# A bidirectional recurrence network on one core: where two conditioning rows are loaded, and which instructions are held to their place

## The chip, the cores and the metric

The kernel runs on one core of one Trainium2 chip. A core has five instruction streams that run beside each other: TensorE (PE, matrix products; its weight loads are listed as PEld), VectorE (DVE), ScalarE (ACT), GpSimd (POOL) and SyncE (SP), which here only issues transfers. Each engine takes its own instructions strictly in the order of the program that was built, and waits at an instruction until the semaphores it names have come. The metric is the device time of one execution in microseconds (us).

## The reference

Two layers of a network are applied to 128 context tokens and 512 latent tokens with the same weights. Context tokens are modulated by the conditioning vector `c_ctx`, latent tokens by `c`. One layer:

```
mod = silu(cond) @ ada_w + ada_b                 # six vectors of 1024: shift, scale, gate, twice
h   = rmsnorm(x, norm_mix) * (1 + sc_m) + sh_m
proj = h @ w_in                                   # 1024 x 4608, nine parts
o   = [4 gated-recurrence heads | 4 retention heads], both directions, head norm, gate
x   = x + g_m * (o @ w_out)
h   = rmsnorm(x, norm_ffn) * (1 + sc_f) + sh_f
gate, up = split(h @ w_up)                        # 1024 x 5632
x   = x + g_f * ((silu(gate) * up) @ w_down)      # 2816 x 1024
```

A final norm follows, and the states of the context tokens are returned. What matters here is the first line: the shifts and scales of both conditionings are 1024 long sums of `silu(cond)` times a column of `ada_w`.

## The kernel before

All 640 tokens stay on the chip. A product in fp32 is made of three products in the rounded type: each weight tile of 128x1024 is loaded raw (`Stream.load`, L65, by SP), its rounded part `wh` is made by ScalarE (L75) and the rest `wl` by VectorE (L76), and TensorE runs wh times the high part of the activations, wh times the low part and wl times the high part. Three raw buffers and four pairs of cut buffers run ahead of TensorE.

The work has stages: an early stage (called the boot here, `ada_first`, traced under a manual schedule, so in the order written), then for each layer the mixer (input projection with the heads' chains between it, `h0`, `a0`, ... in `ORDER`), `w_out`, and the FFN: eleven pairs of `w_up` units, the `w_down` product for 512 columns (L1053 to L1055) twice, eleven more pairs, `w_down` again.

The boot computes the first layer's first shift and scale, because nothing can start without them. Its steps: `load(i)` brings four tiles of `ada_w` (0.5 MB each) for i = 0 to 3; `cut(i, j)` splits tile j (L344 on ScalarE, L345 on VectorE); `mm(i, ..)` multiplies them with the two silu'd vectors (L355, or L358 unsplit); `rt(i)` turns the row to columns (L369), `fin(i)` adds the bias on VectorE (L376). Beside it the tokens are normalized: `xs`, `tr` (eight transposes, L586), `xc` (L395, a copy by ScalarE), then `full` (L408 and L410, scale and shift) and `split` (L414 and L415) make the activations `hT`, half by half, and the first projection products (`gw`, L624 to L626) run between.

All other shifts and scales come from `ada_cols`, for (layer 0, second norm) during layer 0's mixer and for layer 1 (both norms) during layer 0's FFN. It does not use TensorE. `ada_rows` loads both conditioning vectors, repeated on 128 partitions, as `srow` (two transfers of 0.5 MB), and ScalarE takes their silu (L515). Then for 16 tiles `adt` of the transposed `ada_w` (0.5 MB each, L527) VectorE runs two multiply-and-sums (L536), one for each conditioning, into one column of `modc`. `ada_cols` is a generator in a lane, `ada`: `Net.run` steps a lane each time the main work has added so much of an estimated cost (3.0 in the mixer, 4.0 in the FFN). A step decides where in the program an instruction is traced. After the boot the compiler's scheduler then orders each engine's stream anew by its own estimates, and may move an instruction ahead of older ones when it takes its inputs as ready. `pin` (`keep_in_program_order`) adds an edge that holds one instruction behind everything traced before it on its engine.

SP's transfers use eight completion semaphores in turn, so an issue also waits until the transfer eight before it has landed.

Of the kernel before, what the change touches and what calls it, by code (L numbers as in the profile page):

```python
# [13 lines left out]
AF = mybir.ActivationFunctionType  # L14
ALU = mybir.AluOpType
AX = mybir.AxisListType

P = 128
DM = 1024
# [36 lines left out]
class Stream:  # L56
# [5 lines left out]
    def load(self):  # L62
        src, kk, nn = self.slots[self.loaded]
        raw = self.net.rawp.tile([P, 1024], F32, tag="raw", name="raw")
        self.net.nc.sync.dma_start(out=raw[:, :kk * nn].rearrange("p (k n) -> p k n", k=kk), in_=src)  # L65
        self.raw[self.loaded] = (raw, kk, nn)
        self.loaded += 1

# [34 lines left out]
class Net:  # L103
# [218 lines left out]
    def ada_first(self):  # L322
# [89 lines left out]
        def split(t, hf):  # L412
            f, hi, lo = views(t, hf)
            nc.scalar.copy(hi, f)  # L414
            V.tensor_tensor(lo, f, hi.bitcast(F32), op=ALU.subtract)  # L415

        load(0)
        for t in range(NT):
            self.load_x(t)
        load(1)  # L420
        for _ in range(3):
            self.W.load()
        load(2)
        self.new_hT()
        for j in range(4):
# [83 lines left out]
    def ada_rows(self):  # L509
        a = self.a  # L510
        self.srow = self.const.tile([P, 2, DM], F32, name="srow")
        self.junk = self.const.tile([P, DM], F32, name="junk")
        for c, src in enumerate((a["c_ctx"], a["c"])):
            self.nc.sync.dma_start(out=self.srow[:, c], in_=bass.AP(src.tensor, src.offset, [[0, P], [1, DM]]))
        self.nc.scalar.activation(self.srow, self.srow, AF.Silu)  # L515

    def ada_cols(self, l, m, alloc):
        V = self.nc.vector
        if self.srow is None:
            self.ada_rows()  # L520
            yield
        tiles = [(which, j) for which in (1, 0) for j in range(KT)]

        def load(which, j):
            w = alloc("adt")
            row = 3072 * m + which * 1024 + j * P
            self.nc.sync.dma_start(out=w[:, :DM], in_=self.a["ada_t"][l, row:row + P])  # L527
            return w
        nxt = load(*tiles[0])
        for i, (which, j) in enumerate(tiles):  # L530
            w = nxt
            if i + 1 < len(tiles):
                nxt = load(*tiles[i + 1])
            yield
            for c in range(2):
                V.tensor_tensor_reduce(out=self.junk, in0=w[:, :DM], in1=self.srow[:, c], scale=1.0, scalar=0.0,  # L536
                                       op0=ALU.mult, op1=ALU.add,
                                       accum_out=self.modc[:, l, m, 1 - which, c, j:j + 1])
            yield
        self.mod_fin(l, m)  # L540

# [740 lines left out]
```

## Time and profile before

| | us |
|---|---|
| median of 3 runs (1847.05 to 1849.16) | 1849.0 |
| the profiled execution, whole | 1847.48 |
| its span, first to last instruction | 1845.7 |
| TensorE busy in the span | 1793.7 (97%) |
| VectorE busy | 1041.3 (56%) |
| ScalarE busy | 712.1 (39%) |

1.78 us of the profiled execution lie outside the span. Rows of the timeline give a start, a length and, in brackets, how long the engine had been idle before and what ended that idle time; a row with xN merges N instructions of one line. Matmuls overlap, so a row's length is more than the distance from one to the next. The stretches (windows) give each engine's busy time in a part of the span, the clock granted to TensorE as a share of 2.4 GHz, the busy share of the transfer engines, and GB/s. TensorE's clock has two levels, 1.2 and 2.4 GHz.

### The profile page before, as it was taken

How to read it: one execution, taken by the hardware profiler on the slowest of the kernel's cores; microseconds unless marked ns; L12 is line 12 of the kernel's file. 1: busy time of each engine (PE TensorE's matmuls, PEld its weight loads, DVE VectorE, ACT ScalarE, POOL GpSimd, SP SyncE). 2: the span in 40 equal slices, each digit the busy share in tenths (PEclk: the TensorE clock that was granted, in tenths of full speed). 3: DMA queues.
4: the chain of work that ended last, by engine and by line, in shares of the span. 5: the costliest groups of instructions: out<-in, count | busy, mean ns of one | idle time of the engine just before them, and what ended most of it. 6: DMA issues, size and time to landing. Idle time of an engine off the chain costs nothing.

```text
span 1845.7 us, 29294 instructions
## 1 busy us (share of the span) xinstructions
PE 1793.7 (97%) x12301; PEld 1719.7 (93%) x12301; DVE 1041.3 (56%) x1614; ACT 712.1 (39%) x1208; POOL 49.1 (3%) x59
## 2 busy tenths in 40 slices
PE   5999999999999999999999999999999999999998
PEld 3799999998999978999899999999899998899988
DVE  3889757864854986222366656587475522323234
ACT  5675645633522211222246555455352221122221
POOL 1000000000000000000000000000000000000000
PEclk7999999999999999999999999999999999999999
DMA  8424223222433654222222121322234322222221
GB/s 288 155 81 152 78 78 112 92 69 69 137 115 117 224 182 140 80 70 75 75 81 72 50 69 53 109 78 89 80 92 126 115 75 75 80 80 69 75 75 58
DMA packets 204612, 184.06 MB, mean 100 GB/s; under 512 B 6736, under 2 KB 172336, under 8 KB 204480
## 3 DMA queue, kind: packets, MB, share of 16 engines
q1 hardware_dynamic: 199584, 179.67, 30.8%
q10 hardware_dynamic: 4640, 2.43, 0.4%
q8 instruction: 96, 1.57, 0.4%
q0 software_dynamic: 256, 0.09, 0.1%
q14 instruction: 36, 0.29, 0.1%
HBM read 177.44 MB, written 4.72 MB: 99 GB/s over the span
## 4 chain that ended last, share of the span: by engine, by line
PE 78%; DVE 10%; DMA 4%; ACT 4%; issue 3%; SPq 1%; POOL 1%; DVEq 0%; POOLq 0%; ACTq 0%
PE gw L634 36%; PE ga L680 5%; PE ga L679 5%; PE ga L678 5%; PE ga L1053 5%; PE ga L1055 4%; PE ga L1054 4%; PE pl L771 3%; DMA adt<-in_ada_t 2%; DVE junk L536 2%; DVE wl L76 2%; PE gw L625 1%; PE gw L624 1%; PE gw L626 1%; PE ga L1032 1%
## 5 line engine op out<-in xcount | busy, mean ns | idle before, releaser
L634 PE MATMUL gw<-hT,wh 128*128 128x320 f32 x3712 | 702.0, 311 | 0.0
L634 PEld LDWEIGHTS gw<-hT,wh 128*128 128x128 f32 x3712 | 581.3, 188 | 1.1
L75 ACT CAST wh<-raw 128x1024 fp32r<-128x1024 f32 (+2 forms) x224 | 231.7, 1035 | 704.4 <-PE gw L634 267.1
L76 DVE TENSOR_TENSOR wl<-raw,wh 128x1024 fp32r<-128x1024 f32 (+2 forms) x224 | 269.4, 1204 | 357.3 <-ACT wh L75 357.1
L634 PE MATMUL gw<-hT,wl 128*128 128x320 f32 x1856 | 423.8, 309 | 0.0
L634 PEld LDWEIGHTS gw<-hT,wl 128*128 128x128 f32 x1856 | 310.4, 188 | 0.1
L678 PE MATMUL ga<-wh,hT 128*128 128x256 f32 x640 | 185.7, 290 | 0.0
L680 PE MATMUL ga<-wh,hT 128*128 128x256 f32 x640 | 181.4, 284 | 0.0
L679 PE MATMUL ga<-wl,hT 128*128 128x256 f32 x640 | 181.4, 283 | 0.0
L1053 PE MATMUL ga<-wh,act 128*128 128x512 f32 x330 | 130.2, 395 | 4.1 <-DVE xa L996 4.1
L1054 PE MATMUL ga<-wl,act 128*128 128x512 f32 x330 | 129.6, 393 | 0.0
L1055 PE MATMUL ga<-wh,act 128*128 128x512 f32 x330 | 128.8, 393 | 0.0
L536 DVE CUSTOM_DVE_ANT_0 junk<-adt,srow 128x1024 f32<-128x1024 f32 x96 | 117.8, 1227 | 18.5 <-DMA adt<-in_ada_t 17.0
L1104 DVE TENSOR_TENSOR sgf<-sgf,gw 128x640 f32<-128x640 f32 x44 | 36.1, 820 | 162.3 <-PE gw L634 162.3
L678 PEld LDWEIGHTS ga<-wh,hT 128*128 128x128 f32 x640 | 122.7, 192 | 0.3
L679 PEld LDWEIGHTS ga<-wl,hT 128*128 128x128 f32 x640 | 122.6, 192 | 0.3
L680 PEld LDWEIGHTS ga<-wh,hT 128*128 128x128 f32 x640 | 122.4, 191 | 0.0
L505 DVE SCALAR_TENSOR_TENSOR acc<-adw,sTt,acc 128x512 f32<-128x512 f32 x112 | 79.6, 747 | 23.0 <-DMA adw<-in_ada_w 22.7
L1053 PEld LDWEIGHTS ga<-wh,act 128*128 128x128 f32 x330 | 62.6, 190 | 18.6 <-DVE xa L996 6.0
L1055 PEld LDWEIGHTS ga<-wh,act 128*128 128x128 f32 x330 | 62.7, 190 | 13.3
L771 PE MATMUL pl<-X 128*128 128x128 f32 x560 | 72.3, 276 | 2.4 <-ACT X L758 2.3
L1054 PEld LDWEIGHTS ga<-wl,act 128*128 128x128 f32 x330 | 62.6, 190 | 12.5
(226 smaller groups left out, 2639.0 us busy)
## 6 DMA issues: line engine op xcount, KB each, us to landing
raw<-in_w_up SPq DMA_DIRECT2D x88, 512.0 KB, 3.8
raw<-in_w_in SPq DMA_DIRECT2D x72, 512.0 KB, 3.7
adt<-in_ada_t SPq DMA_DIRECT2D x48, 512.0 KB, 4.0
raw<-in_w_down SPq DMA_DIRECT2D x38, 512.0 KB, 3.7
adw<-in_ada_w SPq DMA_DIRECT2D x64, 256.0 KB, 2.9
adw<-in_ada_w SPq DMA_DIRECT2D x16, 512.0 KB, 7.0
raw<-in_w_out SPq DMA_DIRECT2D x16, 512.0 KB, 3.5
gate<-in_ada_b SPq DMA_DIRECT2D x8, 512.0 KB, 5.2
```

The source lines that it names most:

```text
L75: nc.scalar.copy(hi[:, :n], raw[:, :n])
L76: nc.vector.tensor_tensor(lo[:, :n], raw[:, :n], hi[:, :n].bitcast(F32), op=ALU.subtract)
L505: nc.vector.scalar_tensor_tensor(d, w, s, d, op0=ALU.mult, op1=ALU.add)
L536: V.tensor_tensor_reduce(out=self.junk, in0=w[:, :DM], in1=self.srow[:, c], scale=1.0, scalar=0.0, op0=ALU.mult, op1=ALU.add, accum_out=se ...
L634: mm(o, w[:, k], self.hT[:, d, k, sl], start=k == 0 and i == 0, stop=k == KT - 1 and i == 2)
L678: mm(o, a_hi, hi[:, j], start=i == 0, stop=False)
L679: mm(o, a_hi, lo[:, j], start=False, stop=False)
L680: mm(o, a_lo, hi[:, j], start=False, stop=i == nk - 1)
L771: nc.tensor.matmul(pl[:, i * P:(i + 1) * P], X[:, TOK + i * P:TOK + (i + 1) * P], X[:, i * P:(i + 1) * P], start=True, stop=True)
L1053: mm(o, a_hi, hi[:, j], start=i == 0, stop=False)
L1054: mm(o, a_hi, lo[:, j], start=False, stop=False)
L1055: mm(o, a_lo, hi[:, j], start=False, stop=i == nk - 1)
```

## The change

The two transfers of the conditioning rows are issued on SP behind the last weight transfer traced so far (`issue_after`, an edge of order and no wait); the lane steps four times instead of once before the silu is traced; the silu and the first of each two multiply-and-sums are pinned.

```diff
--- before.py
+++ after.py
@@ -62,7 +62,7 @@
     def load(self):
         src, kk, nn = self.slots[self.loaded]
         raw = self.net.rawp.tile([P, 1024], F32, tag="raw", name="raw")
-        self.net.nc.sync.dma_start(out=raw[:, :kk * nn].rearrange("p (k n) -> p k n", k=kk), in_=src)
+        self.last = self.net.nc.sync.dma_start(out=raw[:, :kk * nn].rearrange("p (k n) -> p k n", k=kk), in_=src)
         self.raw[self.loaded] = (raw, kk, nn)
         self.loaded += 1
 
@@ -511,14 +511,16 @@
         self.srow = self.const.tile([P, 2, DM], F32, name="srow")
         self.junk = self.const.tile([P, DM], F32, name="junk")
         for c, src in enumerate((a["c_ctx"], a["c"])):
-            self.nc.sync.dma_start(out=self.srow[:, c], in_=bass.AP(src.tensor, src.offset, [[0, P], [1, DM]]))
-        self.nc.scalar.activation(self.srow, self.srow, AF.Silu)
+            with self.tc.issue_after(self.W.last.ins):
+                self.nc.sync.dma_start(out=self.srow[:, c], in_=bass.AP(src.tensor, src.offset, [[0, P], [1, DM]]))
 
     def ada_cols(self, l, m, alloc):
         V = self.nc.vector
         if self.srow is None:
             self.ada_rows()
-            yield
+            for _ in range(4):
+                yield
+            self.pin(self.nc.scalar.activation(self.srow, self.srow, AF.Silu))
         tiles = [(which, j) for which in (1, 0) for j in range(KT)]
 
         def load(which, j):
@@ -533,9 +535,11 @@
                 nxt = load(*tiles[i + 1])
             yield
             for c in range(2):
-                V.tensor_tensor_reduce(out=self.junk, in0=w[:, :DM], in1=self.srow[:, c], scale=1.0, scalar=0.0,
-                                       op0=ALU.mult, op1=ALU.add,
-                                       accum_out=self.modc[:, l, m, 1 - which, c, j:j + 1])
+                r = V.tensor_tensor_reduce(out=self.junk, in0=w[:, :DM], in1=self.srow[:, c], scale=1.0, scalar=0.0,
+                                           op0=ALU.mult, op1=ALU.add,
+                                           accum_out=self.modc[:, l, m, 1 - which, c, j:j + 1])
+                if c == 0:
+                    self.pin(r)
             yield
         self.mod_fin(l, m)
 
```

In the built program SP issues the same 396 rows, ScalarE has two more table loads (11 for 9), and VectorE the same instructions in another order. Lines of the kernel after it are higher by up to four: L536 is L538 there, L715 is L719, L996 is L1000. TensorE's order differs at some 120 matmuls.

ScalarE in the boot, before: the end of the second `cut`s, the silu of `srow`, the copy `xc(4)`, `cut(1, 3)`, the first cut of a `w_in` tile, and the row of `mm(1, ..)`.

```order
L344 CAST ahi<-adw 128x1024 x2
L515 ACTIVATE srow<-srow 128x2048
L395 COPY xt<-pt 128x1024
L344 CAST ahi<-adw 128x1024
L75 CAST wh<-raw 128x1024
L363 COPY row<-pr 4x512
```

The same place after:

```order
L344 CAST ahi<-adw 128x1024 x2
L395 COPY xt<-pt 128x1024
L344 CAST ahi<-adw 128x1024
L75 CAST wh<-raw 128x1024
L363 COPY row<-pr 4x512
```

The silu has left this place; it now stands some 80 instructions further, in the chain of head `h0`, between two copies of that chain (L791), with a table load ahead of it and one for the sigmoid (L719) behind:

```order
L791 COPY A<-pl 32x5x32 x4
L523 ACT_TABLE_LOAD
L523 ACTIVATE srow<-srow 128x2048
L791 COPY A<-pl 64x5x64 x2
L75 CAST wh<-raw 128x1024
L719 ACT_TABLE_LOAD
L719 ACTIVATE F<-gw 128x640
```

VectorE in the second half of the boot, before: `fin(3)` (L376), scale and shift (L410) and the low parts of `hT` (L415), with multiply-and-sums between.

```order
L536 ISA junk,modc<-adt,srow 128x1024
L536 ISA modc 128x1
L536 ISA junk,modc<-adt,srow 128x1024
L536 ISA modc 128x1
L376 TENSOR_TENSOR modc<-pc,adab 128x2x4
L410 TENSOR_SCALAR xt<-xt,modc 128x128 x6
L536 ISA junk,modc<-adt,srow 128x1024
L536 ISA modc 128x1
L415 TENSOR_TENSOR hT<-xt,hT 128x4x128
L410 TENSOR_SCALAR xt<-xt,modc 128x128 x2
```

The same place after:

```order
L376 TENSOR_TENSOR modc<-pc,adab 128x2x4
L410 TENSOR_SCALAR xt<-xt,modc 128x128 x6
L415 TENSOR_TENSOR hT<-xt,hT 128x4x128
L410 TENSOR_SCALAR xt<-xt,modc 128x128 x2
L415 TENSOR_TENSOR hT<-xt,hT 128x4x128
```

Eight multiply-and-sums have left the boot and the cuts behind it; ten were traced ahead of head `h1`'s chain before and two are now, and all 32 of layer 0's mixer are done at the same later place in both (the second retention head).

VectorE at the first `w_down` of layer 0, before: the product's result `ga` is taken by L996 (`xa`), which frees its PSUM buffer.

```order
L536 ISA junk,modc<-adt,srow 128x1024
L536 ISA modc 128x1
L318 TENSOR_TENSOR modc<-modc,adab 128x8 x2
L320 SCALAR_TENSOR_TENSOR modc<-modc,cols 128x8 x2
L536 ISA junk,modc<-adt,srow 128x1024
L536 ISA modc 128x1
L76 TENSOR_TENSOR wl<-raw,wh 128x1024
L996 TENSOR_TENSOR xa<-ga,gate 128x512
L536 ISA junk,modc<-adt,srow 128x1024
L536 ISA modc 128x1
L998 TENSOR_TENSOR x<-x,xa 128x512
L996 TENSOR_TENSOR xa<-ga,gate 128x512 x2
```

The same place after:

```order
L538 ISA junk,modc<-adt,srow 128x1024
L538 ISA modc 128x1
L538 ISA junk,modc<-adt,srow 128x1024
L538 ISA modc 128x1
L76 TENSOR_TENSOR wl<-raw,wh 128x1024
L1000 TENSOR_TENSOR xa<-ga,gate 128x512
L1002 TENSOR_TENSOR x<-x,xa 128x512
L1000 TENSOR_TENSOR xa<-ga,gate 128x512 x2
L1002 TENSOR_TENSOR x<-x,xa 128x512 x2
L1000 TENSOR_TENSOR xa<-ga,gate 128x512 x2
```

The 64 multiply-and-sums of layer 0's FFN no longer stand in one dense stretch around this product (three or four between two cuts of `wl`), but about two to a `w_up` unit up to the end of the FFN; between the first and last `xa` of this product stand none.

## Rows read from the trace of the kernel before

**Rows 1.** page, part 1: busy us, share of the span, instructions

```profile
PE 1793.7 (97%) x12301; PEld 1719.7 (93%) x12301; DVE 1041.3 (56%) x1614; ACT 712.1 (39%) x1208; POOL 49.1 (3%) x59
```

**Rows 2.** ScalarE by time, early stage: start us, us, line, operation [idle before <- releaser]

```profile
36.97 1.91 ACT L515 ACTIVATE srow<-srow 128x2048 f32<-128x2048 f32 x1 [10.47 <-DMA srow<-in_c]
38.78 0.99 ACT L395 COPY xt<-pt 128x1024 f32<-128x1024 f32 x1
39.68 1.05 ACT L344 CAST ahi<-adw 128x1024 fp32r<-128x1024 f32 x1
```

**Rows 3.** TensorE by time, 26 to 59 us

```profile
26.71 1.91 PE L586 MATMUL pt<-ident,xn 128*128 128x128 f32 x8
...
30.69 0.39 PE L355 MATMUL pr<-alo,sr 128*128 128x512 f32 x1
40.77 0.80 PE L355 MATMUL pr<-ahi,sr 128*128 128x512 f32 x1 [9.70 <-ACT ahi L344]
...
44.35 1.86 PE L369 MATMUL pc<-sel,row 4*128 4x2 f32 x8 [0.66 <-ACT row L363]
46.14 5.64 PE L358 MATMUL pr<-adw,sTt 128*2 128x512 f32 x8
...
53.34 3.59 PE L358 MATMUL pr<-adw,sTt 128*2 128x512 f32 x8
...
58.49 1.05 PE L369 MATMUL pc<-sel,row 2*128 2x2 f32 x8
```

**Rows 4.** issues of SyncE by time, 26 to 30 us

```profile
26.91 0.74 SPq L514 DMA_DIRECT2D srow<-in_c_ctx  x1
27.69 0.43 SPq L514 DMA_DIRECT2D srow<-in_c  x1
```

**Rows 5.** five us stretches: length, busy of each engine, clock, DMA share, GB/s

```profile
30.00:35.00 5.00, 1.08 (x5) 0.56 (x3) 0.00 (x0) 0.00 (x0) 0.00 (x0) 0.82 1.04 394
45.00:50.00 5.00, 5.00 (x11) 1.73 (x12) 4.63 (x12) 3.46 (x9) 0.00 (x0) 0.50 0.03 9
```

**Rows 6.** VectorE by time, 68 to 74 us

```profile
68.98 1.22 DVE L536 CUSTOM_DVE_ANT_0 junk<-adt,srow 128x1024 f32<-128x1024 f32 x1
...
71.88 1.22 DVE L536 CUSTOM_DVE_ANT_0 junk<-adt,srow 128x1024 f32<-128x1024 f32 x1
```

**Rows 7.** TensorE by time, 74 to 76 us

```profile
74.87 0.39 PE L625 MATMUL gw<-hT,wh 128*128 128x256 f32 x1 [1.28 <-DVE hT L415]
```

**Rows 8.** TensorE by time, first w_down stage of each layer

```profile
641.01 0.39 PE L1053 MATMUL ga<-wh,act 128*128 128x512 f32 x1
...
679.76 0.80 PE L1053 MATMUL ga<-wh,act 128*128 128x512 f32 x1 [4.10 <-DVE xa L996]
...
723.80 0.75 PE L634 MATMUL gw<-hT,wh 128*128 128x320 f32 x4
...
1530.53 0.39 PE L1053 MATMUL ga<-wh,act 128*128 128x512 f32 x1
...
1606.63 0.75 PE L634 MATMUL gw<-hT,wh 128*128 128x320 f32 x4
```

**Rows 9.** VectorE by time, 676 to 680 us

```profile
676.73 1.23 DVE L536 CUSTOM_DVE_ANT_0 junk<-adt,srow 128x1024 f32<-128x1024 f32 x1 [1.48 <-DMA adt<-in_ada_t]
...
677.88 1.22 DVE L76 TENSOR_TENSOR wl<-raw,wh 128x1024 fp32r<-128x1024 f32 x1
679.02 0.69 DVE L996 TENSOR_TENSOR xa<-ga,gate 128x512 f32<-128x512 f32 x1
```

**Rows 10.** page, part 5, one group: busy us, mean ns | idle before, releaser

```profile
L536 DVE CUSTOM_DVE_ANT_0 junk<-adt,srow 128x1024 f32<-128x1024 f32 x96 | 117.8, 1227 | 18.5 <-DMA adt<-in_ada_t 17.0
```

**Rows 11.** one stretch of layer 0's mixer, columns as in Rows 5

```profile
160.00:320.00 160.00, 157.62 (x1210) 156.83 (x1209) 116.11 (x191) 84.30 (x155) 6.28 (x5) 1.00 0.33 104
```

**Rows 12.** ScalarE by time, a table load and what follows it

```profile
82.35 1.28 ACT L715 ACT_TABLE_LOAD   x1
83.64 0.71 ACT L715 ACTIVATE F<-gw 128x640 f32<-128x640 f32 x1
```

## The prediction

> **What bounds the kernel now.** I read the shares of the engines first: TensorE is busy 1793.7 of 1845.7 us and VectorE 56% [rows 1]. So a gain can only come from the 52 us in which TensorE is idle and from stretches in which its clock is low, and the question is which wait ends last there. The windows show two such places that the change touches, and the timelines show their causes.
>
> The first is the boot. ScalarE stood 10.47 us until the second conditioning row had landed, took 1.91 us for its silu, and only at 38.78 came to the copy `xc(4)` and at 39.68 to `cut(1, 3)` [rows 2]. TensorE ran dry after its product at 30.69 and stood 9.70 us for that cut [rows 3]. The rows were issued last, at 26.91 and 27.69, behind every tile that the boot needs [rows 4], while the transfer engines were full (share 1.04 at 394 GB/s in 30 to 35) [rows 5]: the silu, which the boot doesn't use, held up the cut. After the standstill TensorE's clock was at 0.50 of full, the lower level of 1.2 GHz, in 45 to 50 [rows 5].
>
> The second is the first `w_down` product of layer 0, which runs from 641.01 to 723.80; the same product in layer 1, where no multiply-and-sum runs, goes from 1530.53 to 1606.63 [rows 8]. That is 82.79 against 76.10 us. Inside it TensorE stood 4.10 us for the first `xa` of VectorE and its next matmul took 0.80 us in place of 0.39 [rows 8]. VectorE was late because a multiply-and-sum at the head of its queue waited 1.48 us for its tile, and a cut of weights ran before the `xa` at 679.02 [rows 9].
>
> **The change, part by part.** All terms are set against the profiled execution (1847.48 us; the median of the three runs lies 1.5 above it).
>
> 1, the silu leaves the boot. `xc(4)` then waits for what else it needs, the transposes, which run from 26.71 for 1.91 us and so end at 28.62 [rows 3]. It can start 38.78 - 28.62 = 10.16 us earlier. Next late could be the tile of `cut(1, 3)`: the issue at 26.91 waits for just that transfer (it stands eight transfers before it) and is through at 27.65 [rows 4], so it is there. The cut would start near 29.5, its VectorE half end near 31.8, and TensorE, free from 31.08 (30.69 + 0.39), waits for that half; the path ScalarE, VectorE, TensorE moves as a whole. The later tiles (`load(2)`, issued ahead of the rows) landed before the rows did, at 36.97 at the latest; the 20 transfers up to their end are 10.5 MB, 26.6 us at 394 GB/s [rows 5], so 28 us at the earliest, and I take 33, between the two; the products that need them come near 34 us. Gain 10.2, between 6.5 (if they land only near 36.97) and 10.2.
>
> 2, the clock. With the idle time gone TensorE need not fall to the low level. `rt(1)` took 1.86 us for eight matmuls, `rt(2)` 1.05; `mm(2)`'s first half took 5.64, its second 3.59 [rows 3]. At the high level throughout this gives back 0.81 + 2.05 = 2.86 us. The engine still has short idle times there (near 31 and 33 us), and the clock was at 0.82 on average in 30 to 35 with 1.08 us of work [rows 5]; so I take half, 1.4, and keep 0 and 2.9 as ends.
>
> 3, the second half of the boot. Without multiply-and-sums VectorE starts `fin(3)` without the one at 68.98 ahead, and the first low part of `hT` without the one at 71.88 [rows 6], 1.22 us each on a path for which TensorE stood 1.28 us [rows 7]. Gain 1.3, between 0 and 1.3, as the wait holds no more.
>
> 4, the multiply-and-sums of the FFN at their place. The five `xa` of the first `w_down` follow each other with one cut of weights among them. Gain 82.79 - 76.10 = 6.7 [rows 8]; one pair (2 x 1.23 us) still stands shortly before the first `xa`, so the low end is 6.7 - 2.5 = 4.2. The later w_up units take the work over: VectorE is idle 44% of the span [rows 1].
>
> 5, what layer 0's mixer gets in return. Eight multiply-and-sums of 1.227 us [rows 10], 9.8 us, go from the boot to the mixer. In 160 to 320 VectorE has 160 - 116.11 = 43.9 us free, and TensorE stands only 2.4 us [rows 11]. ScalarE gets the silu (1.91) [rows 2] and two more table loads of 1.28 [rows 12], 4.5 us, of 75.7 free there. Head chains need both engines in order, so a little may reach TensorE. Ends: 14.3 lost (all of it on the path), or 2.4 won (the waits in that stretch vanish). I take 2.0 lost, near the end that the free time speaks for.
>
> A table load stands without a gap: 82.35 + 1.28 = 83.63, and the sigmoid starts at 83.64 [rows 12]. The Trainium skill, "ScalarE: Activation LUTs", What ACT_TABLE_LOAD costs, has the same load but adds a drain of about 1.38 us to every switch; two switches would be 5.3 us by that and 2.6 by the row, and my sum would lose at most 2.7 more. The row shows no such gap, so I keep the row.
>
> 6, the transfers. The two rows move from the full stretch to the mixer, where the share is 0.33 [rows 11]; SP's issues take 0.74 and 0.43 us [rows 4] and nothing on TensorE's path waits behind them: raw weights run three tiles ahead. Taken as 0; its ends are 1.2 lost (both issues on the path) and 1.2 won (the boot's own issues come earlier by the same).
>
> Sum: 10.2 + 1.4 + 1.3 + 6.7 - 2.0 = 17.6; 1847.48 - 17.6 = 1829.9. I predict 1830 us.
>
> **Rivals.**
>
> A, the clock stays up. If TensorE keeps 2.4 GHz from 31 us on, term 2 is 2.9 and the last product of `mm(1)` is faster too; about 1828. For it: the standstill of 9.7 us goes. Against it: two short gaps stay. The Trainium skill, "TensorE: Matmul & The Clock Gate", Part 1, says that the clock is throttled by default and activity releases it, which speaks for this; the trace agrees in so far as the clock is at 0.50 after the standstill [rows 5].
>
> B, the mixer takes the gain back. The moved VectorE work and ScalarE's loads meet the head chains: 14.3 lost in place of 2.0, so 1842.2. For it: a chain passes between the two engines step by step, and the eight come into the middle of such chains. Against it: 43.9 us of VectorE free in 160 to 320 [rows 11].
>
> C, slower: a pinned multiply-and-sum blocks VectorE while its tile is on the way. Before, the scheduler could run cuts of weights ahead of it; now one stands at the head of the queue 32 times in layer 0's FFN. Place: the w_up units behind 585 us. Price: 1.48 us of wait [rows 9] each time it reaches TensorE. The first `w_down` then keeps its loss (term 4 gone), so 10.9 are left to lose, and it decides from 10.9 / 32 = 0.34 us for each tile pair. At every other of the 32 it is 23.7: 1847.5 - 10.9 + 23.7 = 1860. Against it: over all 96 the waits for tiles were 17.0 us [rows 10], 0.18 each, and weights are cut up to four tiles ahead.
>
> D, the change doesn't do what it says in the boot. If `cut(1, 3)`'s tile or `load(2)` only lands near 36.97 with the queue so full, ScalarE starts about 2.7 us earlier than at 39.68 and no more: 2.7 + 1.3 + 6.7 - 2.0 = 8.7, 1838.8. Against it: the issue that was through at 27.65.
>
> **How the numbers follow.** Forecast 0.55, A 0.20, B 0.10, D 0.08, C 0.07. 0.2% of 1849 is 3.7 us, about what a measurement of this kernel can tell from no change. Forecast, A and D are faster by more (0.83); B at 1842.2 is so in most of its spread, two thirds, and same in the rest; C is slower, with a little near nothing. So faster 0.90, same 0.04, slower 0.06. The range: best, all terms at their good ends, 10.2 + 2.9 + 1.3 + 6.7 + 2.4 = 23.5, 1824; towards the bad side it takes in D and most of B, to 1842. C is left out, and the rest of B.
>
> **What would show it.** Right: no row of the silu among ScalarE's first 40 us, `xc(4)` near 28.7 us and TensorE's gap of 9.70 us gone; `mm(2)` near 34 us; no `junk` row before 110 us; the first `w_down` of layer 0 in 76 to 79 us with no 4.10 us wait; TensorE's waits in the mixer within 2 us of now. Wrong: TensorE waiting for a transfer of `ada_w` at 31 to 37 us (D); longer idle times ahead of the head chains' matmuls, released by VectorE or ScalarE (B); multiply-and-sums whose wait for a tile adds up to much over 17.0 us, with cuts of weights late behind them (C).

## The result and the profile after

The changed kernel took 1829.48 us (median of 4 runs, 1828.59 to 1830.5), the kernel before 1848.03 beside it: a ratio of 0.99, 95% interval 0.9883 to 0.9917, so 18.6 us faster, with 15.3 to 21.6 as the interval. The profiled execution took 1828.59, its span 1826.8.

The page of the changed kernel, first TensorE's busy time, then the multiply-and-sums (columns as in [rows 1, 10]):

```profile
PE 1787.0 (98%) x12301; PEld 1714.3 (94%) x12301; DVE 1041.3 (57%) x1614; ACT 714.6 (39%) x1210; POOL 50.8 (3%) x59
...
L538 DVE CUSTOM_DVE_ANT_0 junk<-adt,srow 128x1024 f32<-128x1024 f32 x96 | 117.2, 1221 | 2.2 <-ACT srow L523 1.1
```

TensorE's idle time in the span fell from 52 to 39.8 us; its busy time fell too, by 6.7, since products at the higher clock are shorter (eight of `mm(2)` take 3.60 in place of 5.64 us, below). VectorE's wait for tiles of `ada_t` is gone: 18.5 us idle ahead of the 96 sums before, 2.2 now.

Where the time came from is read by setting the start of the same TensorE instruction in one trace against that in the other. The program was also profiled a second time (`after_again`, below), so there are two columns of gain:

| instruction, its start before | changed | gain | again | gain |
|---|---|---|---|---|
| a product ahead of the standstill, 28.84 | 26.91 | 1.9 | 28.46 | 0.4 |
| second product behind it, 42.04 | 30.15 | 11.9 | 31.54 | 10.5 |
| second eight of `mm(2)`, 53.34 | 38.62 | 14.7 | 40.98 | 12.4 |
| product behind the boot's last wait, 75.10 | 58.71 | 16.4 | 61.08 | 14.0 |
| first product of `w_out`, 420.04 | 408.32 | 11.7 | 410.66 | 9.4 |
| first `w_down` product, 641.01 | 629.31 | 11.7 | 631.67 | 9.3 |
| first `w_up` product behind it, 721.53 | 703.10 | 18.4 | 705.43 | 16.1 |

So the boot gave 14 to 16 us, layer 0's mixer took 4.7 back, the first `w_down` gave 6.7, and nothing else in 1827 us moved by more than 0.5. The columns differ in the boot only. The 1.9 of the first line lies ahead of anything that the change touches: it is a difference between executions, as the 0.4 of the same program in the second shows.

ScalarE at the place where it had stood [rows 2], in the changed kernel:

```profile
26.88 1.01 ACT L395 COPY xt<-pt 128x1024 f32<-128x1024 f32 x1 [0.47 <-PE pt L590]
27.80 1.04 ACT L344 CAST ahi<-adw 128x1024 fp32r<-128x1024 f32 x1
```

`xc(4)` starts at 26.88 in place of 38.78, 0.47 us after the engine came free, and `cut(1, 3)` follows at 27.80. The silu is at 106.55. TensorE in the same stretch, to be read against [rows 3]:

```profile
28.89 0.50 PE L355 MATMUL pr<-ahi,sr 128*128 128x512 f32 x1
30.15 0.50 PE L355 MATMUL pr<-alo,sr 128*128 128x512 f32 x1 [0.76 <-DVE alo L345]
...
31.78 1.05 PE L369 MATMUL pc<-sel,row 4*128 4x2 f32 x8 [0.67 <-ACT row L363]
32.76 3.60 PE L358 MATMUL pr<-adw,sTt 128*2 128x512 f32 x8
...
38.62 3.60 PE L358 MATMUL pr<-adw,sTt 128*2 128x512 f32 x8
```

The 9.70 us of standstill are gone; 0.76 and 0.67 are left. No wait took its place. The eight of `rt(1)` after it take 1.05 us (1.86 before) and the eight of `mm(2)` 3.60 (5.64 before). The same rows in the second execution of the same program:

```profile
33.17 1.05 PE L369 MATMUL pc<-sel,row 4*128 4x2 f32 x8 [0.66 <-ACT row L363]
34.15 5.27 PE L358 MATMUL pr<-adw,sTt 128*2 128x512 f32 x8
...
40.98 3.60 PE L358 MATMUL pr<-adw,sTt 128*2 128x512 f32 x8
```

Here the first eight of `mm(2)` take 5.27. Stretches of 5 us, first of the one execution, then of the other (columns as in [rows 5]):

```profile
30.00:35.00 5.00, 4.18 (x17) 1.96 (x18) 3.49 (x8) 2.44 (x5) 0.00 (x0) 1.00 1.05 385
35.00:40.00 5.00, 4.64 (x20) 1.99 (x18) 4.52 (x13) 4.87 (x11) 0.00 (x0) 1.00 1.03 374
```

```profile
30.00:35.00 5.00, 4.31 (x18) 2.42 (x18) 3.26 (x3) 2.70 (x4) 0.00 (x0) 0.84 1.05 388
35.00:40.00 5.00, 5.00 (x13) 1.27 (x12) 4.56 (x15) 4.40 (x10) 0.00 (x0) 0.74 0.53 171
```

The clock stayed at full speed in the one; in the other it was at 0.84 and 0.74 on average, which is part of the time at the lower of its two levels. The instructions are the same, and the idle time before them (0.66 us) is no longer. The two clocks had differed before that, ahead of anything that the change moves: in 25 to 30 us it was 1.00 in the one execution and 0.50 in the other.

The first `w_down` of both layers in the changed kernel answers to [rows 8]:

```profile
629.31 0.39 PE L1057 MATMUL ga<-wh,act 128*128 128x512 f32 x1
...
705.37 0.74 PE L638 MATMUL gw<-hT,wh 128*128 128x320 f32 x4
...
1512.10 0.39 PE L1057 MATMUL ga<-wh,act 128*128 128x512 f32 x1
...
1588.14 0.75 PE L638 MATMUL gw<-hT,wh 128*128 128x320 f32 x4
```

That is 705.37 - 629.31 = 76.06 us in layer 0 and 1588.14 - 1512.10 = 76.04 in layer 1: the loss of 6.7 against the layer without sums is gone, and so is the wait of 4.10 us.

What the mixer took back shows in TensorE's waits: its product, the releaser, us in total, times, longest; the changed kernel, then before:

```profile
PE pl L775 <- ACT X L762: 4.9, 5, 1.7
```

```profile
PE pl L771 <- ACT X L758: 2.3, 3, 1.3
```

The products `pl` of the head chains wait 4.9 us for the copies `X`, 2.3 before. How such a wait comes about is seen in three engines, VectorE, then ScalarE, then TensorE:

```profile
147.37 0.83 DVE L779 TENSOR_TENSOR QQ<-QQ,F 128x640 f32<-128x640 f32 x1
148.11 1.23 DVE L538 CUSTOM_DVE_ANT_0 junk<-adt,srow 128x1024 f32<-128x1024 f32 x1
...
149.25 0.83 DVE L780 TENSOR_TENSOR KK<-KK,F 128x640 f32<-128x640 f32 x1
```

```profile
150.12 0.72 ACT L762 COPY X<-KK 128x640 f32<-128x640 f32 x1 [1.15 <-DVE KK L780]
```

```profile
150.90 1.27 PE L775 MATMUL pl<-X 128*128 128x128 f32 x9 [1.67 <-ACT X L762]
```

The chain step is QQ, then KK, each followed by its copy on ScalarE. A sum (`junk`, 148.11, the second of a pair whose first is pinned) stands between the two, KK starts 1.88 us behind QQ in place of 0.74, its copy waits 1.15 us and TensorE 1.67.

This wait shows the mechanism, but it is not where the mixer's time went. A little later TensorE had stood 1.56 us for `S` before, and in the changed kernel it does not:

```profile
188.69 0.49 PE L815 MATMUL po<-S,QQ 128*128 128x128 f32 x2 [1.56 <-DVE S L824]
```

The gain, read at points where TensorE has done the same products in both kernels, shows the places. At starts before of 75.10, 157.98, 199.09, 205.88, 224.90 and 420.04 us it is 16.4, 16.3, 16.2, 14.0, 14.3 and 11.7. So only 0.2 us are lost up to 199.09, and the silu, its two table loads and the wait at 150.90 all lie in that stretch. Then 2.1 are lost between 199.09 and 205.88, and 2.5 behind 224.90.

The first of these losses is at a retention head. ScalarE makes four copies `SW` for it, before in a row; in the changed kernel the fourth comes 4.9 us behind the third (179.87), with a cut of weights and four steps of a gate between. The rows are those of before, then of after:

```profile
192.65 4.22 ACT L862 COPY SW<-QR 32x1024 f32<-32x1024 f32 x4
```

```profile
184.73 1.04 ACT L866 COPY SW<-QR 32x1024 f32<-32x1024 f32 x1
```

VectorE's `QR` needs all four, so it is late, and TensorE waits for it and for the `kTr` made from it. Neither wait was there before:

```profile
189.48 1.16 PE L879 MATMUL pa<-QR 128*128 128x128 f32 x8 [0.93 <-DVE QR L872]
...
191.85 2.05 PE L898 MATMUL pur<-vb,kTr 128*128 128x128 f32 x16 [0.78 <-ACT kTr L892]
```

The second loss is at `pl` again. One KK starts at 213.93, 3.76 us behind its QQ (210.17). Between them stand a step `on` of another head, which waited 1.06 us for GpSimd, and a sum:

```profile
212.79 1.22 DVE L538 CUSTOM_DVE_ANT_0 junk<-adt,srow 128x1024 f32<-128x1024 f32 x1
```

```profile
215.57 1.38 PE L775 MATMUL pl<-X 128*128 128x128 f32 x10 [1.17 <-ACT X L762]
```

This `pl` comes 6.08 us behind the one ahead of it (209.49), before 4.44 (222.65 and 227.09).

### The profile page after: what moved, and what is told of

Its sections match the earlier page's. It is cut to its first block, busy times and chain, and to the rows that moved or that the text cites. A ratio compares the mean times of both kernels' runs of the same rounds, so it can differ in the third digit from the quotient of the medians.

```text
span 1826.8 us, 29296 instructions
## 1 busy us (share of the span) xinstructions
PE 1787.0 (98%) x12301; PEld 1714.3 (94%) x12301; DVE 1041.3 (57%) x1614; ACT 714.6 (39%) x1210; POOL 50.8 (3%) x59
## 4 chain that ended last, share of the span: by engine, by line
PE 82%; DVE 9%; ACT 4%; issue 2%; DMA 1%; POOL 1%; SPq 0%; DVEq 0%; POOLq 0%; ACTq 0%
PE gw L638 39%; PE ga L1057 5%; PE ga L1059 5%; PE ga L1058 5%; PE ga L684 5%; PE ga L683 5%; PE ga L682 5%; PE pl L775 3%; DVE wl L76 1%; DMA adw<-in_ada_w 1%; PE gw L629 1%; PE gw L628 1%; PE gw L630 1%; ACT wh L75 1%; PE ga L1036 1%
## 5 line engine op out<-in xcount | busy, mean ns | idle before, releaser
L538 DVE CUSTOM_DVE_ANT_0 junk<-adt,srow 128x1024 f32<-128x1024 f32 x96 | 117.2, 1221 | 2.2 <-ACT srow L523 1.1
L1057 PEld LDWEIGHTS ga<-wh,act 128*128 128x128 f32 x330 | 61.9, 188 | 14.3 <-DVE xa L1000 1.9
L775 PEld LDWEIGHTS pl<-X 128*128 128x128 f32 x560 | 67.8, 191 | 7.7 <-ACT X L762 7.1
```

Of the source, the lines that this page charges most:

```text
L538: r = V.tensor_tensor_reduce(out=self.junk, in0=w[:, :DM], in1=self.srow[:, c], scale=1.0, scalar=0.0, op0=ALU.mult, op1=ALU.add, accum_ou ...
L775: nc.tensor.matmul(pl[:, i * P:(i + 1) * P], X[:, TOK + i * P:TOK + (i + 1) * P], X[:, i * P:(i + 1) * P], start=True, stop=True)
L1057: mm(o, a_hi, hi[:, j], start=i == 0, stop=False)
```

## The experiments

Those below the first two rows are timed in five rounds against the kernel before on the same chip (medians of before there 1847.1 to 1847.9). The three stretches are starts of TensorE rows: the first `pl` of the head chains; from there to the first product of `w_out` (the mixer); from the first `w_down` product to the first `w_up` product behind it (the row of [rows 8] that ends the stretch there comes some 2.3 us later, so that 82.79 is 80.5 here). "mm(2)" is the length of its first eight products.

| run | median us | ratio (95%) | first `pl` | mixer | `w_down` | mm(2) |
|---|---|---|---|---|---|---|
| before | 1848.0 | 1 | 95.70 | 324.3 | 80.5 | 5.64 |
| changed | 1829.5 | 0.9883-0.9917 | 79.32 | 329.0 | 73.8 | 3.60 |
| e1_pin_ffn | 1829.6 | 0.9889-0.9916 | 79.81 | 327.2 | 73.8 | 3.60 |
| e2_silu_only | 1833.8 | 0.9919-0.9944 | 80.03 | 327.2 | 79.0 | 3.60 |
| e3_pins_only | 1844.9 | 0.9979-0.9996 | 94.19 | 329.8 | 73.8 | 5.52 |
| e4_rows_behind | 1835.1 | 0.9919-0.9946 | 80.90 | 327.9 | 79.3 | 3.60 |
| e5_silu_pin | 1831.1 | 0.9896-0.9924 | 81.97 | 328.9 | 73.9 | 5.29 |
| e6_spread | 1847.6 | 0.9989-1.0007 | 81.66 | 343.6 | 73.8 | 3.60 |
| e7_eight_short | 1827.2 | 0.9875-0.9906 | 80.61 | 325.5 | 73.8 | 3.60 |
| e8_boot_silu | 1829.3 | 0.9887-0.9915 | 86.26 | 323.3 | 73.8 | 3.60 |
| e10_spread_fast | 1844.3 | 0.9978-0.9996 | 81.79 | 343.3 | 73.8 | 5.29 |
| e11_boot_silu_spread | 1840.9 | 0.9956-0.9980 | 80.54 | 339.2 | 73.8 | 3.60 |
| after_again | 1830.1 | 0.9897-0.9924 | 81.69 | 329.0 | 73.8 | 5.27 |
| e12_boot_silu_first | 1830.2 | 0.9885-0.9918 | 81.58 | 328.7 | 73.8 | 5.29 |

**Where the mixer's 4.7 us go.**

```diff
-                if c == 0:
+                if c == 0 and l == 1:
```

> The pin stays on the multiply-and-sums of layer 0's FFN (32 of 48 pinned pairs); the 16 pairs of layer 0's mixer are left to the scheduler again. Theory P (place): the 4.6 us that TensorE lost in the mixer come from pinned multiply-and-sums standing between the two products of a head chain; then the mixer's loss falls under 1.5 us, the boot (16.4) and the first w_down (6.7) stay as in the changed kernel, and the time is 1825 to 1826.5 us. Rival W (work): the loss comes from the eight multiply-and-sums, the silu and the table loads that the mixer gets in any case; then the loss stays and the time is 1828.5 to 1830.5.

The mixer took 327.2: 1.8 of the 4.7 are the place, 2.9 are not. Neither theory holds alone, though the time, 1829.6, lies in the rival's range and not in P's. By the places above, the 2.5 us behind 224.90 are gone, the 2.1 at `QR` are not, and 1.1 are lost ahead of them, where TensorE now waits 1.36 us for `S` at 173.63. The place is seen in the same chain step of this run, VectorE and then TensorE:

```profile
148.32 0.82 DVE L779 TENSOR_TENSOR QQ<-QQ,F 128x640 f32<-128x640 f32 x1
149.06 0.82 DVE L780 TENSOR_TENSOR KK<-KK,F 128x640 f32<-128x640 f32 x1
149.79 1.22 DVE L538 CUSTOM_DVE_ANT_0 junk<-adt,srow 128x1024 f32<-128x1024 f32 x1
```

```profile
150.69 1.38 PE L775 MATMUL pl<-X 128*128 128x128 f32 x10 [0.61 <-ACT X L762]
```

The sum now stands behind QQ and KK, and TensorE waits 0.61 in place of 1.67.

**The silu without any pin on the sums.**

```diff
-                if c == 0:
-                    self.pin(r)
```

> Rows behind the weights and silu pinned, no multiply-and-sum pinned. Boot as in the changed kernel (first product of layer 0's mixer 16.4 us earlier than before). The first w_down of layer 0 takes its 82.8 us of before again if the pin alone is what mends it: 6.7 us more than the run with the pin in the FFN only, 1832 to 1833 us by theory P, 1835 to 1837 by W. Rival F: the w_down product gains without the pin too, since the sums run later anyway; then within 1.5 us of the run with the pin in the FFN only.

1833.8, 4.3 more than with the FFN pins (`w_down` stretch 79.0 against 73.8). So rival F is out: without the pins most of the loss comes back, 5.2 us of it here. It is the one of [rows 9] again, VectorE and then TensorE:

```profile
663.29 1.23 DVE L538 CUSTOM_DVE_ANT_0 junk<-adt,srow 128x1024 f32<-128x1024 f32 x1 [1.53 <-DMA adt<-in_ada_t]
...
664.44 1.22 DVE L76 TENSOR_TENSOR wl<-raw,wh 128x1024 fp32r<-128x1024 f32 x1
665.58 0.68 DVE L998 TENSOR_TENSOR xa<-ga,gate 128x512 f32<-128x512 f32 x1
```

```profile
666.32 0.72 PE L1055 MATMUL ga<-wh,act 128*128 128x512 f32 x1 [3.53 <-DVE xa L998]
```

A sum waits 1.53 us for its tile, the cut of weights comes ahead of `xa`, and TensorE stands 3.53 us. VectorE's order in this FFN is that of the kernel before, so the sums' place does not explain that the stretch is 1.5 us shorter than before (80.5). The wait is 0.6 shorter (3.53 for 4.10), and the granted clock was at 1.00 again 3.7 us behind the wait (670 to 674 us), where before it was at 0.85 still in 684 to 688, from 4.2 us behind it on.

**The pins alone.** Rows and silu are as before the change, so the diff to the kernel before is:

```diff
-                V.tensor_tensor_reduce(...)
+                r = V.tensor_tensor_reduce(...)
+                if c == 0:
+                    self.pin(r)
```

> The kernel before with the pins on the multiply-and-sums alone; rows and silu as before, in the boot. The parts are independent: boot unchanged (ScalarE waits some 10 us for the row, first product near 80 us), first w_down 76 to 77 us; mixer's loss in part (0 to 4.6, by P most of it): 1841 to 1846 us. Rival: pinned sums behind a silu that waits for its row hold VectorE in the boot too, over 1848.

1844.9, inside the range. ScalarE and TensorE in its boot:

```profile
37.23 1.91 ACT L520 ACTIVATE srow<-srow 128x2048 f32<-128x2048 f32 x1 [10.18 <-DMA srow<-in_c]
```

```profile
41.04 0.80 PE L355 MATMUL pr<-ahi,sr 128*128 128x512 f32 x1 [9.42 <-ACT ahi L344]
```

The standstill is there (9.42) and `mm(2)` is slow (5.52). `w_down` is short (73.8): the pins alone take away the whole 6.7. The mixer lost 5.4 although silu and its table loads were not in it, 2.1 of that between 199.09 and 205.88 as in the changed kernel. From the product at 73.21 us before to the first `pl` it took 21.1 us, before 22.5: without sums there this piece is 1.4 shorter, here by the pins alone.

**One half of the change in the boot at a time.** First the rows behind the weights, with silu and sums unpinned:

```diff
-            for _ in range(4):
-                yield
-            self.pin(self.nc.scalar.activation(self.srow, self.srow, AF.Silu))
+            self.nc.scalar.activation(self.srow, self.srow, AF.Silu)
+            yield
```

> Only the order of the two row transfers (behind the last weight transfer), silu and multiply-and-sums left to the scheduler. If the transfer's place is what decides, the scheduler itself puts the silu behind the boot: boot as in the changed kernel, and the time is that of the run without pins on the sums, within 2 us. Rival: the silu stands late in the boot or early in the mixer and waits for its rows there; then a wait of ScalarE over 1 us stands before the silu's row and the time is over 1838 us.

The silu left the boot with no pin on it, presumably since the scheduler now takes its input as late. It went to 86.94, behind a wait:

```profile
85.65 1.28 ACT L521 ACT_TABLE_LOAD   x1 [2.40 <-DMA srow<-in_c]
86.94 1.91 ACT L521 ACTIVATE srow<-srow 128x2048 f32<-128x2048 f32 x1
```

2.40 us of ScalarE are lost there: the rival's wait came, its time of over 1838 did not. The time is 1.3 over the run above without pins on the sums, less than either run scatters (1832.1 to 1836.6 and 1833.0 to 1837.0). Then the other half, the silu pinned and the rows at their old place:

```diff
-            with self.tc.issue_after(self.W.last.ins):
-                self.nc.sync.dma_start(...)
+            self.nc.sync.dma_start(...)
```

> The changed kernel with the two row transfers back at their old place (ahead of the weights of the boot's end); silu and sums pinned as in the changed kernel. If the transfers' place is worth nothing by itself (theory, term 6 of the prediction), the boot is within 0.6 us of the changed kernel's and the time 1828.5 to 1831 us. Rival: rows in the full queue delay a tile that the boot needs; TensorE then waits for a transfer between 26 and 45 us, by up to the 2.7 us that 1 MB takes at 394 GB/s: up to 1832.

1831.1, just over the upper edge of the first theory's range. The boot was not within 0.6 us of the first execution of the changed kernel (first `pl` 81.97 against 79.32), but this execution had the slow `mm(2)` (5.29); against the second one, which had it too, it is 0.3 longer (81.69). TensorE waited for no transfer in the boot. Either half takes the silu out; the place of the transfers by itself shows as 1.6 us against the first timing of the changed kernel (1831.1 - 1829.5) and as 0.9 against the second (1830.1).

**The sums further apart.**

```diff
             yield
+            if l == 0:
+                yield
         self.mod_fin(l, m)
```

> The changed kernel with the 16 pairs of layer 0's mixer half as dense again (three steps of the side lane for a pair in place of two, from 108 us to past 300). Measured from the first product of the head chains to the first product of w_out, before takes 324.3 us, the changed kernel 329.0, the kernel with the pin in the FFN only 327.2. Theory D (density: each pinned sum on VectorE makes a chain late only where VectorE has no slack, 120 to 250 us): 326 to 327.5 us, time 1826.5 to 1828.5. Rival S (every pinned sum costs the same wherever it stands): 329 and 1829.5 as now. Rival G (the sums run into the gates' work from 290 us on): over 330 and over 1831.

Up to 300 us the mixer lost 0.9 us where the changed kernel lost 4.4, which is what density predicts. The 0.9 is a balance: 1.8 were won up to 199.09, 2.2 lost at `QR`, and 0.4 behind. Then it lost 18 more up to `w_out`. Two issues of SP that follow each other on the tiles `adt`, and TensorE behind the gates:

```profile
299.55 0.34 SPq L529 DMA_DIRECT2D adt<-in_ada_t  x1
...
360.46 0.42 SPq L529 DMA_DIRECT2D adt<-in_ada_t  x1
```

```profile
423.08 0.80 PE L565 MATMUL pg<-hl,onesr 128*128 128x512 f32 x1 [15.87 <-ACT hl L561]
```

Between the issue at 299.55 and the one at 360.46 no tile of `ada_t` was asked for; the gates, next in the lane, came 15.87 us too late for `w_out`. I had expected the gates to be squeezed, but by a microsecond or two.

**The eight sums from the boot.** On the kernel with the pin in the FFN only:

```diff
+            n = DM if l or i > 3 else 32
...
-                r = V.tensor_tensor_reduce(out=self.junk, in0=w[:, :DM], in1=self.srow[:, c], ...
+                r = V.tensor_tensor_reduce(out=self.junk[:, :n], in0=w[:, :n], in1=self.srow[:, c, :n], ...
```

> The kernel with the pin in the FFN only, where the first eight sums of the mixer take 32 of the 1024 columns (that part of the computation is left out, so its time is a probe). The mixer of that kernel takes 2.9 us more than before without any pin. Theory W (the eight sums that came from the boot are the cost): stretch back to 324.3 to 325.3 us, time 1826.5 to 1827.5. Rival T (the silu and its two table loads on ScalarE are the cost): stretch 327 and time 1829 as in the kernel with the pin in the FFN only.

The mixer took 325.5: the length of the eight sums is 1.7 of the 2.9 us, 1.2 are left. They lie at `QR`: up to 199.09 this run even wins 0.6, then it loses the same 2.1.

**The silu as the boot's last step.** The rows are issued behind `load(3)`, mask and rope, and in the boot's list:

```diff
         out.append(lambda: split(NT - 1, 1))
+        out.append(lambda: nc.scalar.activation(self.srow, self.srow, AF.Silu))
```

> The row transfers issued behind load(3), mask and rope in the boot, the silu written as the boot's last ScalarE step (its table is still loaded there, its rows have landed), sums pinned in the FFN only; the mixer's sums can begin in the boot's tail as before. By the terms measured so far: boot as in the changed kernel or up to 1.4 us longer (a sum on VectorE ahead of the last low part of hT), the mixer's stretch back at 324.3 to 326, first w_down short: 1825 to 1828 us, faster than the changed kernel. Rival: the silu's 1.9 us delay the cut of weights or the first gate at 62 us and the rows' 1 MB the boot's last tiles; then 1829 to 1831.

1829.3, as the changed kernel. The silu ran without a wait and without a load of its own:

```profile
63.52 1.91 ACT L490 ACTIVATE srow<-srow 128x2048 f32<-128x2048 f32 x1
```

and the mixer from the first `pl` took 323.3, but the first chain started 6.5 us later than with the pin in the FFN only (86.26 against 79.81), 4.3 of it behind the boot. TensorE there:

```profile
82.66 1.35 PE L762 MATMUL pd<-QS 128*128 128x128 f32 x10 [2.77 <-DVE z L273]
```

Five sums, free to run at once, stand on VectorE between 70 and 84 us, ahead of or between the first chain's steps, and the chain's first product waited 2.77 us for VectorE. VectorE also stood 2.79 us there for a result `u` of GpSimd (up to 75.43), which the run with the pin in the FFN only does not; which share each has is not separated. The cost moved from the middle of the mixer to its start.

**A finer pace.** Three steps for a pair, the lane stepped every 2.5 units:

```diff
-Q_ADA = (3.0, 2.0, 4.0)
+Q_ADA = (2.5, 2.0, 4.0)
```

> The changed kernel with three steps for a pair as in the run that spread the sums, and the side lane stepped every 2.5 units in place of 3.0, so that a pair comes every 7.5 units (6.0 in the changed kernel, 9.0 in the spread run) and the gates behind the sums are done some 18 us ahead of w_out. Theory D (density): the mixer's stretch (329.0 us in the changed kernel, 0.9 us lost up to 300 us in the spread run) comes down to 325 to 327; time 1826 to 1828. Rival: the gates, now denser between 300 and 390 us, cost there what is won: 328 to 330, no faster than the changed kernel beside it.

The same with the silu appended to the boot's list as above:

> As the run before it, and the silu as the boot's last ScalarE step with the rows behind load(3), mask and rope, so that the mixer has neither the silu nor its two table loads, while the sums stay pinned at their places behind 100 us. If silu and loads cost the 1.2 us of the mixer that the short sums left open: stretch 1.2 us shorter than in the run before it, 1825 to 1827. Rival (ScalarE has room for them): the same within 0.5 us, and a boot longer by up to 2 us, 1826 to 1830.

And the changed kernel unedited:

> The changed kernel beside the two others on the same chip: 1828.5 to 1831 us; the boot (first product of the first head's transform of hT) within 1.5 us of 58.2, TensorE's clock at full from 31 us on if rival A of the prediction holds in every run.

The changed kernel came out as expected but for its boot (2.4 us longer, above) and its clock, which was not at full speed throughout. The two others were slower than it, by 14 and 11 us; neither theory had that. Issues of `adt` in the first of them:

```profile
233.29 4.92 SPq L529 DMA_DIRECT2D adt<-in_ada_t  x2
...
371.77 0.33 SPq L529 DMA_DIRECT2D adt<-in_ada_t  x1
```

From 238 to 372 us none was issued, with a quarter of the pairs left. The tiles come from a pool of four buffers that also holds the heads' outputs `on`; once those stand in it, the rest of the lane waits for the heads. That is read from the code and fits the issues; a larger pool was not tried. Up to 270 us the mixer lost 5.2 with the silu in it and 2.3 without, in two programs whose sums stand in about the same places. That would speak for the silu as part of the cost, but in the changed kernel itself the silu costs TensorE at most 0.1 us: the gain is 16.4 at 75.10 and 16.3 at 157.98, with the silu in between.

**The silu's place alone.** As with the silu in the boot, with the first sum pinned so that none runs ahead of the first chain:

```diff
-                if c == 0:
+                if c == 0 and (l == 1 or i == 0):
```

> The silu as the boot's last ScalarE step (rows behind load(3), mask and rope), the sums of layer 0's mixer free except the first, which is pinned so that none runs in the boot or ahead of the first chain; FFN sums pinned. Set against the kernel with the pin in the FFN only, which differs by the silu's place alone: theory T (silu and table load cost the mixer's chains what the short sums left open, 1.2 us, or up to 2.9 as the two spread runs differ by up to 270 us): stretch 324.4 to 326, time 1826 to 1828, faster than the changed kernel. Rival W (the sums alone cost): stretch 327, 1829 to 1831.

328.7, more than the 327.2 of the run with the pin in the FFN only, which speaks against theory T. (The two differ by the place of the rows and by the pin on the first sum too.) ScalarE and TensorE at the place of the loss:

```profile
114.08 1.28 ACT L718 ACT_TABLE_LOAD   x1
...
118.09 1.01 ACT L802 COPY kT<-pk 128x1024 f32<-128x1024 f32 x1
```

```profile
119.15 3.09 PE L807 MATMUL pu<-va,kT 128*128 128x128 f32 x16 [2.11 <-ACT kT L802]
```

The room that the silu left was taken by other table work; the copy `kT` came at 118.09 (114.93 in that other run, whose chains start 1.8 us earlier), and TensorE waited 2.11 for it. No version that does the whole computation beat the changed kernel.

The last 1.2 us of the mixer have a place, as the kept traces show: between the two products that start at 199.09 and 205.88 before, all thirteen traces of edited kernels lose 2.0 to 2.2 us, whether sums are pinned or not, long or short, and wherever the silu stands; up to 0.5 comes back a little later. In each of them the fourth copy `SW` comes 4.8 us or more behind the third, and TensorE waits 0.9 to 1.0 us for `QR` and 0.8 for `kTr`. So this loss hangs neither on the silu nor on the sums' place or length; it goes with the scheduler's order of those copies, which in every edited program is not that of before. That the order causes it is read from what TensorE waits for: no run held the copies in their old order, and why the scheduler moved the fourth stays open.

## Why the prediction was right, and where its sizes were off

It said 1830 (1824 to 1842) and the time is 1829.5; each term can be set against the gains above.

- Term 1, the silu leaves the boot: 10.2, measured 10.0 and 10.1 in the two executions (11.9 - 1.9, 10.5 - 0.4). The tile of `cut(1, 3)` had landed, as read from the issue at 26.91 [rows 4], so rival D did not happen. The run with the pins alone keeps the standstill, and each half of the change removes it.
- Term 2, the clock: 1.4 of 2.9, taken as half. Between 42.04 and 53.34 the gain is 2.8 in one execution and 1.9 in the other. Rival A, the clock stays up, is neither right nor wrong: of 12 profiled executions with the silu out of the first 40 us, 8 ran the first eight of `mm(2)` in 3.6 us and 4 in 5.3; both with the silu in front ran them in 5.5 to 5.6. The rule cited there, "TensorE: Matmul & The Clock Gate" of the Trainium skill, Part 1 (throttled unless there is activity), agrees with the 0.50 behind the standstill [rows 5]; it does not tell the 8 from the 4.
- Term 3, the second half of the boot: 1.3, measured 1.4 between the last first-half product and the boot's end, plus 0.3 before it; the run with the pins alone shows the same 1.4.
- Term 4, the FFN: 6.7, measured 6.7, and by the pins alone 6.7 too (80.5 to 73.8). Rival C (a pinned sum blocks VectorE) did not happen: VectorE waits 2.2 us over all 96 sums.
- Term 5, the mixer: 2.0 lost, measured 4.7. This is the mis-sized term, and the sign set for it failed: TensorE's idle time in the mixer rose from 7.8 to 10.9 us, by more than 2. I judged it by VectorE's free time over 160 us [rows 11], 43.9 us, and by the eight sums that moved. But 0.2 us were lost up to 199.09, where the silu and the first of the moved sums run. The loss came in two places that the average hides: 2.1 at `QR`, by the scheduler's order of ScalarE's copies, and 2.5 behind 224.90, where pinned sums stand within the head chain. VectorE's busy time does not tell this, even in a short stretch. The changed kernel, where the second loss is, and the same work with the pin in the FFN only, where it is not (columns as in [rows 5]):

```profile
205.00:230.00 25.00, 23.40 (x182) 22.43 (x181) 23.70 (x37) 12.75 (x28) 1.68 (x1) 1.00 0.33 106
```

```profile
206.00:231.00 25.00, 24.94 (x202) 24.67 (x201) 23.44 (x37) 13.20 (x22) 1.17 (x1) 1.00 0.27 85
```

  VectorE is busy 23.70 and 23.44 of 25 us, but TensorE is idle for 1.60 and 0.06. What differs is where on VectorE the sums stand: two of them between a QQ and its KK in the one, none in the other. Part of this is rival B's mechanism, at a third of its price.
- Term 6, the transfers: 0, between -1.2 and 1.2; the run that put them back was 0.9 to 1.6 slower, and its boot 0.3 longer where both traces had the slow `mm(2)`.

The mechanism of the boot and of the FFN was right. That the sum came within 0.4 us is in part luck, because two errors cancel: the mixer 2.7 too good; the boot 1.1 (again) to 3.5 (first execution) too small, of which 0.4 to 1.9 lie ahead of the change.

## What to carry to other kernels

An instruction that waits for a late transfer blocks everything behind it on its engine (here ScalarE for 10.47 us); look for the consumer that the stage does not need, and either delay its input's issue or pin it: one sufficed here. Work moved off an idle stretch lands somewhere: judge the landing place by the step of the chain that it will stand ahead of, since busy time did not tell it, neither over 160 us nor over 25. A pin fixes a place, so choose that place against the chain that runs there: the same pin gained 6.7 us in the FFN and lost 1.8 in the mixer. And an edit can cost time where it changes nothing itself, by the order that the scheduler then makes: set two traces against each other at points where the same work is done, and read the loss where the difference moves, not at the longest wait.

## Not expected of the hardware

The clock granted to TensorE for the same instructions was not the same in each execution: 1.00 in 30 to 40 us in one, 0.84 and 0.74 in the other, whose idle times in that stretch were no longer. Ahead of it they differed somewhat: the wait before one product of `mm(1)` near 25 us was 0.86 and 1.16 us, and the clock in 25 to 30 us 1.00 and 0.50. In `mm(2)` that is 1.7 us on eight products (3.60 and 5.27). The two boots of one program differ by 2.4 us by this and by the early stage, so half of a term of that size can't be read from one trace.
